# Row sums of squares on TensorE, and first projections begun block by block, in a two-layer hybrid diffusion step

## The chip, the cores and the metric

One NeuronCore of one Trainium2 chip runs the whole program. The metric is the time of one execution on the device in microseconds (us). The engines are named as in the profile: PE is TensorE (PEld its weight loads), DVE is VectorE, ACT is ScalarE, POOL is GpSimd, SP is the engine whose queue issues most of the DMA transfers.

## The reference, cut to what matters

The program is one inference step of a two-layer backbone on 640 tokens (512 latent, 128 context) of width 1024. Each layer starts with

```python
h = rmsnorm(x, prm['norm1_g'][l]) * (1 + sc1) + sh1      # sc1, sh1: slices of silu(cond) @ w_mod + b_mod
cols = jnp.einsum('bnd,de->bne', h, prm['w_in'][l])       # 2832 columns: q, k, v, z, logits, u, vb, pp
# rmsnorm: x * rsqrt(mean(x * x over the 1024 features) + eps) * g
```

and goes on with a gated DeltaNet, a spatial-gating MLP and a pooling branch on slices of `cols`, an output projection, a second norm of the same kind and a SwiGLU FFN. A last norm follows the second layer. Only the first norm of the first layer and the first products behind it are touched here.

## The kernel before, in words

Features lie on the 128 partitions, tokens on the free axis: `xall` holds x as 8 blocks of 128 features x 640 tokens (KT = 8 blocks, NCH = 5 chunks of 128 tokens). float32 products are made as three products of operands split in a rounded part (hi) and a rest (lo): `mm3` issues hi x hi, hi x lo and lo x hi, all through the helper `mm` (L117). The 16 columns of the logits (C_L) need only two products per block, since hi and lo of their weights share one operand. DVE's helpers are `tt` (L122), `stt` (L125) and `ts`; ACT's is `act` (L150).

The norm is applied late. `Norm.add` (L403 to L411) makes block k of x times (gain x (1 + scale)) as `xhi` on ACT and `xlo` on DVE; the products run on that, and each product is multiplied by the row factor `rst` = 1 / sqrt(mean square) as it leaves PSUM. The shift of the modulation rides along as two extra columns in front (`Norm.shift`, L396), so the first half of a product (320 tokens and these two columns) needs the shift, and the second half does not.

The start of the program does this. x is loaded, transposed on PE (L547), positions are added. Then the row statistics: ACT squares the 8 blocks (L580, L582), DVE adds the odd ones into `sb` (L584) and POOL the even ones into `nrm.ss` (L586), and one DVE add joins the two (L587); later `rstd` turns this sum over with five PE transposes (L430), reduces it on DVE (L431) and takes the inverse root. Beside that, the scale half of the modulation is made in two halves of 512 columns (`first_mod_`, L499): 8 float32 products of 32 output rows by 512 columns, placed in four column groups of the array so that four can run side by side; a copy out of PSUM on DVE (`msb`, L505), four PE transposes (L508), a reduce (L510) and two small DVE operations to `sc1` (L591). The first half of the modulation (columns of blocks 0 to 3) is followed in the program by `add` of blocks 0 to 3, the second by `add` of blocks 4 to 7.

Until the shift is there, `early` (L631 to L636) makes the second halves (320 tokens) of four products that do not carry it: logits and first key block, k = 0 to 7, then second key block and first query block, k = 0 to 7. Their weights come from `lgb`, `k0b` and, split at L622 and L623 with a low priority, `k1b` and `q0b`. Then come the row factor (`finish`, L437), the two halves of the shift modulation (L640), the shift columns (L642), and the first halves of the same four products, in `gemm_xs`.

The order of each engine's queue is fixed before the run. A planner takes the instructions by priority (program order, moved by the entries of PRI through `at`) as they become ready in its own account of time; a negative entry means later: `first` +1000, `rst` +80, `add` -100, `kept` -1000. On the chip each engine then runs its queue in that order.

```python
with at("add"):
    nrm.add(k, xks[k], None, shift=False)
```

Of the kernel before, what the change touches and what calls it, by code (L numbers as in the profile page):

```python
# [9 lines left out]
F32 = mybir.dt.float32  # L10
# [6 lines left out]
D = 1024  # L17
P = 128
# [14 lines left out]
# steps of the modulation after each half of a product, by branch  # L33
PUMPS = {'log0': (0, 0), 'k00': (0, 0), 'q00': (1, 2), 'sgu0': (1, 1), 'z0': (0, 1), 'v10': (1, 1), 'q10': (0, 0), 'v00': (1, 0), 'k10': (0, 1), 'pool0': (1, 0)}
# engines of single steps: a ScalarE, v VectorE, p GpSimdE
ENG = {"gul11": "a", "kd10": "a", "conv_k01": "a", "conv_v10": "v", "gul00": "v", "mtc10": "v", "pumpmix0": "a", "kd11": "v", "gul01": "v", "mtc01": "a", "conv_q00": "v", "conv_v00": "v", "kd00": "a", "conv_q10": "a", "conv_k00": "v", "conv_q11": "a", "conv_v01": "a", "conv_v11": "a", "gul10": "a", "kn11": "a", "kn01": "a", "msb": "v", "pumpout0": "a", "dec01": "a", "conv_k11": "a", "dec00": "s", "pumpffn0": "a", "mtc11": "v", "mtc00": "a", "kd01": "a"}
GW, NB = 3, 2
# offsets in the order of issue: > 0 earlier
# [7 lines left out]
def host_constants():  # L46
# [10 lines left out]
    # from here on: not kept on chip as they are  # L57
# [34 lines left out]
def tile_hybrid_step(ctx: ExitStack, tc: tile.TileContext,  # L92
# [40 lines left out]
    def times(key, o, i, c, default):  # L133
        """o = i * c, c one number per row"""
        e = ENG.get(key, default)
        if e == "a":
            act(o, i, AF.Copy, scale=c)
        elif e == "v":
            ts(o, i, c, None, MUL)
        else:  # L140
            nc.gpsimd.tensor_scalar(o, i, c, None, op0=MUL)
# [10 lines left out]
    class at:  # L152
        """the instructions inside come that much earlier in the order of issue"""
# [11 lines left out]
    def behind(ins, prev):  # L165
        """queues one instruction of an engine behind another"""
# [10 lines left out]
    def in_turn(key, ins):  # L177
        """instructions of one kind in the order of the program"""
# [40 lines left out]
    # steps: 512 columns x 128 rows of w_mod; a step's load is issued some steps ahead of its arithmetic  # L219
# [4 lines left out]
    def mod_sums(l, c0, ma):  # L224
# [11 lines left out]
        # sums over the 32 rows of each quarter, then over the quarters  # L236
# [50 lines left out]
    def pump_to(l, w):  # L287
        """until that sixth of the modulation is there"""
# [8 lines left out]
    def wload(parts, kn, n):  # L297
        """parts: [(dram [rows, n], k0, kn)] -> [P, kn, n]"""
# [7 lines left out]
    def wsplit(v):  # L306
        """hi, lo as blocks [P, n]"""
# [32 lines left out]
    def mmk(o, wb, k, xk, sl):  # L340
        """one k block of the products with the scaled residual; 16 columns: hi and lo in one operand"""
# [6 lines left out]
    def gemm_xs(wb, xs, evac, pumps=(1, 1), done=None):  # L348
        """products with the scaled residual; the first half carries two shift columns in front.
        done: the second half's, where it came first."""  # L350
# [28 lines left out]
    def rsqrt(y, a, t):  # L379
        """y = 1 / sqrt(a) for small tiles: bit shift, then three Newton steps; t: scratch like y."""  # L380
# [8 lines left out]
    class Norm:  # L389
        """scaled residual split in two, and the row statistics of the plain one."""  # L390
# [33 lines left out]
        def rstd(self, after=None):  # L424
            """per row: [row in chunk, chunk]"""
            st = sm.tile([P, 3, NCH], F32, tag="st", name="st", bufs=2)
            for q0, q1 in ((4, 5), (0, 4)):
# [5 lines left out]
            ts(st[:, 1], st[:, 1], 1.0 / D, EPS, MUL, ADD)  # L433
# [3 lines left out]
        def finish(self, after=None):  # L437
            r = self.rstd(after)
# [17 lines left out]
    wsp = tc.alloc_tile_pool(name="wsh", bufs=1, side="right")  # L456
    with tc.tile_pool(name="xin", bufs=1) as xp:
# [27 lines left out]
        def first_w(pool, j, c0, kp=KT):  # L485
            """512 columns of w_mod; the row blocks from kp on in the tiles of the later steps"""
# [7 lines left out]
        def first_mod(ws, c0, pool=None):  # L494
            """four row blocks side by side"""
# [40 lines left out]
        # feature rows, positions added  # L536
# [34 lines left out]
        sb = sm.tile([P, NT], F32, tag="rst", name="sb", bufs=1)  # L571
        for k in range(KT):
            xk = xks[k]
            if k % 2:
                sq = xp.tile([P, NT], F32, tag="sq", name="sq", bufs=1)
            else:
                sq = sm.tile([P, 2, 512], F32, tag="ma", name="sq", bufs=1).rearrange("p s n -> p (s n)")[:, 0:NT]
            # sums of squares in two strands
            if k < 2:
                act((nrm.ss, sb)[k], xk, AF.Square)  # L580
                continue
            act(sq, xk, AF.Square)  # L582
            if k % 2:
                tt(sb, sb, sq, ADD)  # L584
            else:
# [851 lines left out]
```

## Time and profile before

| | |
|---|---|
| median of 3 runs | 1740.75 us (1739.99 to 1743.5) |
| span of the profiled execution, first to last instruction | 1737.7 us |
| PE busy | 1666.4 us (96%) |
| DVE, ACT, POOL busy | 1155.2, 761.1, 585.3 us |
| mean granted clock of PE | 0.987 of full |
| DMA | 174.34 MB, mean 100 GB/s |

The page gives the span of the profiled execution and no separate time for it; the median of the runs stands 3.05 us above that span. Times in the rows are microseconds from the span's start: start, duration, engine, line, operation, output <- inputs, shapes and how many instructions were merged; in brackets the idle time before and what ended it. A clock of 1.00 is 2.4 GHz, 0.50 is 1.2 GHz.

### The profile page before, as it was taken

What the parts mean: (1) busy time and instruction counts of PE and PEld (TensorE: products, weight loads), DVE (VectorE), ACT (ScalarE), POOL (GpSimd) and SP (SyncE); (2) the same over time, 40 slices, a digit from 0 to 9 for tenths busy, and PEclk for the clock granted to TensorE, in tenths of its full rate; (3) what the DMA queues carried; (4) which work ended last, traced back from release to release, by engine and by line L of the source; (5) the groups of instructions that cost most, each with busy time, mean ns of one, the idle gap of its engine ahead of it and who ended that gap; (6) DMA issues with size and microseconds to landing.
All of it is one profiled execution on the core that took longest, in us unless ns stands there. A gap on an engine that the chain in (4) does not pass through costs nothing.

```text
span 1737.7 us, 33153 instructions
## 1 busy us (share of the span) xinstructions
PE 1666.4 (96%) x12952; PEld 1603.2 (92%) x12952; DVE 1155.2 (66%) x2462; ACT 761.1 (44%) x1564; POOL 585.3 (34%) x578
## 2 busy tenths in 40 slices
PE   6999999998899999999999999999999999999997
PEld 4788989988899999999998899999999999999997
DVE  6698688799888688877467777675544434433454
ACT  4557765554444344434246656543322212321232
POOL 3342330367645454554164112013411221222110
PEclk8999999999999999999999999999999999999999
DMA  9431231444444544453241211113222222222221
GB/s 316 143 98 57 68 99 29 150 127 139 145 141 141 154 137 143 143 158 103 62 144 52 62 38 50 37 51 126 83 73 74 79 79 74 74 73 73 74 85 61
DMA packets 243379, 174.34 MB, mean 100 GB/s; under 512 B 10006, under 2 KB 212376, under 8 KB 243224
## 3 DMA queue, kind: packets, MB, share of 16 engines
q1 hardware_dynamic: 231888, 157.44, 29.8%
q10 hardware_dynamic: 10184, 12.29, 2.2%
q0 software_dynamic: 1152, 2.51, 0.4%
q8 instruction: 102, 1.67, 0.4%
q14 instruction: 53, 0.43, 0.1%
HBM read 163.29 MB, written 8.91 MB: 99 GB/s over the span
## 4 chain that ended last, share of the span: by engine, by line
PE 53%; DVE 3%; ACT 1%; issue 1%; POOL 0%; DMA 0%; DVEq 0%; POOLq 0%; ACTq 0%
PE acc L117 47%; PE dl L117 5%; DVE wl L122 0%; PE md L117 0%; DMA w<-in_w_down_dram 0%; PE dl L1379 0%; DVE cv L125 0%; POOL guh L830 0%; PE md L760 0%; DVE yt L125 0%; DVE st L125 0%; DVE Z L122 0%; ACT wh L322 0%; ACT MT L945 0%; DVE SI L122 0%
## 5 line engine op out<-in xcount | busy, mean ns | idle before, releaser
L117 PE MATMUL acc<-xhi,wh 128*128 128x322 f32 (+2 forms) x2112 | 667.4, 316 | 5.4 <-DVE ga L122 4.6
L117 PE MATMUL acc<-xlo,wh 128*128 128x322 f32 (+2 forms) x2112 | 666.0, 316 | 1.4 <-DVE xlo L125 1.2
L117 PE MATMUL acc<-xhi,wl 128*128 128x320 f32 (+1 forms) x2080 | 655.0, 315 | 5.1 <-DVE wl L122 5.1
L326 POOL TENSOR_TENSOR wl<-w,wh 128x384 fp32r<-128x384 f32 x188 | 258.7, 1376 | 792.5 <-ACT wh L322 777.9
L117 PEld LDWEIGHTS acc<-xhi,wh 128*128 128x128 f32 (+1 forms) x2112 | 399.4, 189 | 10.7 <-PE acc L117 7.2
L117 PEld LDWEIGHTS acc<-xlo,wh 128*128 128x128 f32 (+1 forms) x2112 | 400.2, 189 | 4.1 <-POOL spp L1148 1.5
L117 PEld LDWEIGHTS acc<-xhi,wl 128*128 128x128 f32 x2080 | 396.4, 191 | 6.6 <-DVE wl L122 5.9
L322 ACT CAST wh<-w 128x1024 fp32r<-128x1024 f32 (+1 forms) x188 | 194.5, 1035 | 343.4 <-PE acc L117 282.6
L282 POOL TENSOR_TENSOR ma<-ma,wm 128x512 f32<-128x512 f32 x140 | 207.2, 1480 | 133.5 <-ACT wm L150 113.8
L122 DVE TENSOR_TENSOR wl<-w,wh 128x640 fp32r<-128x640 f32 (+1 forms) x188 | 213.3, 1134 | 50.5 <-ACT wh L322 23.9
L117 PE MATMUL acc<-ah,wh 128*128 128x320 f32 (+2 forms) x632 | 195.6, 309 | 0.7 <-ACT ah L1322 0.7
L117 PE MATMUL acc<-al,wh 128*128 128x320 f32 (+2 forms) x632 | 195.1, 309 | 0.1
L117 PE MATMUL acc<-ah,wl 128*128 128x320 f32 (+2 forms) x632 | 195.1, 309 | 0.0
L150 ACT ACTIVATE wm<-wm,sc 128x512 f32<-128x512 f32 x140 | 101.1, 723 | 135.0 <-DVE ma L125 117.8
L125 DVE SCALAR_TENSOR_TENSOR x<-acc,mod,x 128x128 f32<-128x128 f32 (+3 forms) x192 | 77.9, 434 | 119.8 <-PE acc L117 119.5
L125 DVE SCALAR_TENSOR_TENSOR ma<-wm,sc,ma 128x512 f32<-128x512 f32 x140 | 134.9, 964 | 25.6 <-DMA wm<-in_w_mod_dram 24.7
L117 PEld LDWEIGHTS acc<-ah,wh 128*128 128x128 f32 x632 | 118.7, 188 | 1.2 <-ACT ah L1322 1.1
L117 PEld LDWEIGHTS acc<-al,wh 128*128 128x128 f32 x632 | 118.7, 188 | 0.3 <-DVE al L122 0.3
L117 PEld LDWEIGHTS acc<-ah,wl 128*128 128x128 f32 x632 | 118.7, 188 | 0.0
L1322 ACT CAST ah<-ga 128x320 fp32r<-128x320 f32 x88 | 40.5, 460 | 155.9 <-DVE ga L125 155.9
L150 ACT ACTIVATE ga<-ga,bt 128x320 f32<-128x320 f32 x132 | 57.4, 468 | 89.9 <-DVE ga L122 89.9
L122 DVE TENSOR_TENSOR ga<-acc,rst 128x320 f32<-128x320 f32 x88 | 42.4, 483 | 73.9 <-PE acc L117 73.4
(369 smaller groups left out, 2481.7 us busy)
## 6 DMA issues: line engine op xcount, KB each, us to landing
w<-in_w_gu_dram SPq DMA_DIRECT2D x88, 512.0 KB, 3.7
wm<-in_w_mod_dram SPq DMA_DIRECT2D x162, 256.0 KB, 2.9
w<-in_w_in_dram SPq DMA_DIRECT2D x44, 512.0 KB, 3.6
w<-in_w_down_dram SPq DMA_DIRECT2D x32, 512.0 KB, 4.2
w<-in_w_out_dram SPq DMA_DIRECT2D x32, 256.0 KB, 3.0
wf<-in_w_mod_dram SPq DMA_DIRECT2D x30, 256.0 KB, 6.5
w<-in_w_down_dram SPq DMA_DIRECT2D x16, 384.0 KB, 3.4
x<-xd ACTq DMA_DIRECT2D x16, 320.0 KB, 4.7
```

Source lines behind the costliest of these rows:

```text
L117: return nc.tensor.matmul(o, lhsT=l, rhs=r, start=st, stop=sp, **kw).ins
L122: recent["v"] = nc.vector.tensor_tensor(o, a, b, op=op).ins
L125: recent["v"] = nc.vector.scalar_tensor_tensor(o, a, s, b, op0=op0, op1=op1).ins
L150: recent["a"] = nc.scalar.activation(o, i, f, **kw).ins
L282: nc.gpsimd.tensor_tensor(ma[:, 1], ma[:, 1], wm, op=ADD)
L322: nc.scalar.copy(wh, v)
L326: nc.gpsimd.tensor_tensor(wl[:, c:], v[:, c:], wh[:, c:], op=SUB)
L1322: nc.scalar.copy(hi[:, sl], ga[:, sl])
```

## The change

The squares are no longer added up elementwise. Each squared block serves as the weights of five float32 products (one for each chunk of 128 tokens) with two columns of ones, all 8 x 5 of them accumulated in one PSUM tile, whose columns then are the row sums in the layout that `rstd` wants; its transposes and reduces fall away for this norm. The second `first_mod` loses its priority of +1000. The products of logits and first key block are issued for k = 0 to 3 between the two halves of the modulation; then second key block and first query block for k = 0 to 3, and both pairs for k = 4 to 7.

```diff
-        def rstd(self, after=None):
+        def rstd(self, after=None, sums=None):
             st = sm.tile([P, 3, NCH], F32, tag="st", name="st", bufs=2)
-            for q0, q1 in ((4, 5), (0, 4)):
+            for q0, q1 in ((4, 5), (0, 4)) if sums is None else ():
...
-            ts(st[:, 1], st[:, 1], 1.0 / D, EPS, MUL, ADD)
+            ts(st[:, 1], st[:, 1] if sums is None else sums, 1.0 / D, EPS, MUL, ADD)
...
-        sb = sm.tile([P, NT], F32, tag="rst", name="sb", bufs=1)
+        pss = dl()[:, 0:2 * NCH]
         for k in range(KT):
-            xk = xks[k]
-            if k % 2:
-                sq = xp.tile([P, NT], F32, tag="sq", name="sq", bufs=1)
-            else:
-                sq = sm.tile([P, 2, 512], F32, tag="ma", name="sq", bufs=1).rearrange("p s n -> p (s n)")[:, 0:NT]
-            if k < 2:
-                act((nrm.ss, sb)[k], xk, AF.Square)
-                continue
-            act(sq, xk, AF.Square)
-            if k % 2:
-                tt(sb, sb, sq, ADD)
-            else:
-                nc.gpsimd.tensor_tensor(nrm.ss, nrm.ss, sq, op=ADD)
-        tt(nrm.ss, nrm.ss, sb, ADD)
+            sq = xp.tile([P, NT], F32, tag="sq", name="sq", bufs=2)
+            act(sq, xks[k], AF.Square)
+            for ch in range(NCH):
+                mm(pss[:, 2 * ch:2 * ch + 2], sq[:, ch * P:(ch + 1) * P], ones[:, 0:2], k == 0 and ch == 0, k == KT - 1 and ch == NCH - 1, skip_group_check=True)
+        ssum = sm.tile([P, NCH], F32, tag="ssum", name="ssum", bufs=1)
+        early = {C_L: (lgb, acc()[0:32, 0:HALF]), C_K: (k0b, acc()[:, 0:HALF])}
+        def early_go(cs, k0, k1):
+            for k in range(k0, k1):
+                for c0 in cs:
+                    mmk(early[c0][1], early[c0][0], k, nrm.xs[k], slice(HALF + 2, XW))
         for j in range(2):
-            first_mod(wsc[j], D + 512 * j, xp)
+            if j == 0:
+                first_mod(wsc[j], D, xp)
+            else:
+                first_mod_(wsc[j], D + 512, xp)
...
                 nc.sync.dma_start(xd[k], xks[k])
+            if j == 0:
+                early_go((C_L, C_K), 0, 4)
+        nc.vector.tensor_copy(ssum, pss.rearrange("p (c t) -> p c t", t=2)[:, :, 0])
...
-                for cs in ((C_L, C_K), (C_K + P, C_Q)):
-                    for k in range(KT):
-                        for c0 in cs:
-                            mmk(early[c0][1], early[c0][0], k, xs[k], slice(HALF + 2, XW))
+                early[C_K + P], early[C_Q] = (k1b, acc()[:, 0:HALF]), (q0b, dl()[:, 0:HALF])
+                early_go((C_K + P, C_Q), 0, 4)
+                early_go((C_L, C_K), 4, KT)
+                early_go((C_K + P, C_Q), 4, KT)
                 with at("rst"):
-                    rst = nrm.finish(split)
+                    rst = nrm.finish(split, ssum)
```

## Rows read from the trace of the kernel before

**Rows 1.** The page: span, and busy time of each engine.

```profile
span 1737.7 us, 33153 instructions
PE 1666.4 (96%) x12952; PEld 1603.2 (92%) x12952; DVE 1155.2 (66%) x2462; ACT 761.1 (44%) x1564; POOL 585.3 (34%) x578
```

**Rows 2.** Windows: PE, PEld, DVE, ACT, POOL busy, then PEclk, DMA share, GB/s.

```profile
20.00:21.00 1.00, 1.00 (x8) 0.00 (x0) 0.55 (x1) 0.42 (x1) 1.00 (x1) 0.53 1.09 345
...
32.00:33.00 1.00, 0.00 (x0) 0.00 (x0) 1.00 (x3) 0.00 (x0) 0.00 (x0) 0.50 0.96 304
...
38.00:39.00 1.00, 1.00 (x9) 0.88 (x8) 1.00 (x3) 1.00 (x4) 0.00 (x0) 1.00 1.03 373
```

**Rows 3.** Timeline of PE from 17 to 56 us.

```profile
17.98 3.36 PE L117 MATMUL md<-wf,sc 128*32 128x512 f32 x16 [1.84 <-ACT sc L150]
22.75 0.66 PE L508 MATMUL md<-r_ident,msb 128*128 128x128 f32 x4 [1.41 <-DVE msb L147]
23.34 4.33 PE L117 MATMUL md<-wf,sc 128*32 128x512 f32 x16
33.41 1.12 PE L508 MATMUL md<-r_ident,msb 128*128 128x128 f32 x4 [5.74 <-DVE msb L147]
...
35.58 0.61 PE L117 MATMUL acc<-xhi,wh 128*32 128x320 f32 x1
...
39.70 0.31 PE L117 MATMUL acc<-xhi,wh 128*32 128x320 f32 x1
...
42.66 0.31 PE L117 MATMUL acc<-xhi,evn 128*128 128x320 f32 x1
...
55.80 0.31 PE L117 MATMUL acc<-xhi,wh 128*32 128x322 f32 x1
```

**Rows 4.** Timeline of DVE, same stretch.

```profile
20.45 1.64 DVE L122 TENSOR_TENSOR sb<-sb,sq 128x640 f32<-128x640 f32 x1 [3.68 <-ACT sq L150]
22.02 0.68 DVE L147 COPY msb<-md 128x512 f32<-128x512 f32 x1
22.90 1.59 DVE L122 TENSOR_TENSOR sb<-sb,sq 128x640 f32<-128x640 f32 x1 [0.20 <-ACT sq L150]
24.41 0.18 DVE L510 TENSOR_REDUCE mod<-md 128x8 f32<-128x32 f32 x1
...
27.77 0.81 DVE L122 TENSOR_TENSOR sb<-sb,sq 128x640 f32<-128x640 f32 x1
...
32.68 0.68 DVE L147 COPY msb<-md 128x512 f32<-128x512 f32 x1
...
35.94 3.79 DVE L125 SCALAR_TENSOR_TENSOR xlo<-xall,sc,xhi 128x512 fp32r<-128x512 f32 x8 [0.52 <-ACT xhi L150]
```

**Rows 5.** Timeline of ACT, same stretch.

```profile
17.82 0.72 ACT L150 ACTIVATE ss<-xall 128x640 f32<-128x640 f32 x1
...
26.25 3.73 ACT L150 ACTIVATE xhi<-xall,sc 128x512 fp32r<-128x512 f32 x8
```

**Rows 6.** Timeline of PE: float32 products alone, narrow ones, and four groups side by side.

```profile
44.07 1.92 PE L117 MATMUL md<-wf,sc 128*32 128x512 f32 x16
...
46.77 1.02 PE L117 MATMUL dl<-ss,cst 128*128 128x512 f32 x2
47.64 0.60 PE L508 MATMUL md<-r_ident,wm 128*128 128x128 f32 x4
...
69.49 0.33 PE L117 MATMUL dl<-g,cst 128*128 128x20 f32 x2
...
70.78 0.40 PE L117 MATMUL acc<-xhi,eon 128*128 128x322 f32 x1
```

**Rows 7.** Window in the first layer's inverse: small products at the lower clock.

```profile
250.50:251.00 0.50, 0.50 (x38) 0.50 (x41) 0.50 (x1) 0.00 (x0) 0.50 (x1) 0.50 0.00 0
```

**Rows 8.** SP's timeline at the last loads for the shift; their time to landing.

```profile
38.10 2.03 SPq L490 DMA_DIRECT2D wm<-in_w_mod_dram  x2
...
DMA to landing us min/median/max: 5.3/5.8/6.2
```

More of the change, by code (lines that the diff above doesn't have):

```diff
@@ L432, in rstd, with finish @@
                                                op=ADD, axis=AX.X).ins, after)
-            ts(st[:, 1], st[:, 1], 1.0 / D, EPS, MUL, ADD)
+            ts(st[:, 1], st[:, 1] if sums is None else sums, 1.0 / D, EPS, MUL, ADD)
             rsqrt(st[:, 0], st[:, 1], st[:, 2])
             return st[:, 0]
-        def finish(self, after=None):
-            r = self.rstd(after)
+        def finish(self, after=None, sums=None):
+            r = self.rstd(after, sums)
             rst = sm.tile([P, NT], F32, tag="rst", name="rst", bufs=1)
@@ L570, in tile_hybrid_step @@
         tt(wsum, wsum, cw3[:, :, 2, :], ADD)
-        sb = sm.tile([P, NT], F32, tag="rst", name="sb", bufs=1)
+        pss = dl()[:, 0:2 * NCH]
         for k in range(KT):
-            xk = xks[k]
-            if k % 2:
-                sq = xp.tile([P, NT], F32, tag="sq", name="sq", bufs=1)
-            else:
-                sq = sm.tile([P, 2, 512], F32, tag="ma", name="sq", bufs=1).rearrange("p s n -> p (s n)")[:, 0:NT]
-            if k < 2:
-                act((nrm.ss, sb)[k], xk, AF.Square)
-                continue
-            act(sq, xk, AF.Square)
-            if k % 2:
-                tt(sb, sb, sq, ADD)
-            else:
-                nc.gpsimd.tensor_tensor(nrm.ss, nrm.ss, sq, op=ADD)
-        tt(nrm.ss, nrm.ss, sb, ADD)
-        for j in range(2):
-            first_mod(wsc[j], D + 512 * j, xp)
+            sq = xp.tile([P, NT], F32, tag="sq", name="sq", bufs=2)
[8 more added lines that the diff above has]
+                    mmk(early[c0][1], early[c0][0], k, nrm.xs[k], slice(HALF + 2, XW))
+        for j in range(2):
+            if j == 0:
+                first_mod(wsc[j], D, xp)
+            else:
+                first_mod_(wsc[j], D + 512, xp)
             with at("first"):
@@ L604, in tile_hybrid_step @@
                 pa_.tile([P, n], F32, tag=tag, name=f"{tag}_", bufs=b)
-            early = {}
             if l == 0:
@@ L630, in tile_hybrid_step @@
                 split = recent["v"]
-                early = {C_L: (lgb, acc()[0:32, 0:HALF]), C_K: (k0b, acc()[:, 0:HALF]),
-                         C_K + P: (k1b, acc()[:, 0:HALF]), C_Q: (q0b, dl()[:, 0:HALF])}
-                for cs in ((C_L, C_K), (C_K + P, C_Q)):
-                    for k in range(KT):
-                        for c0 in cs:
-                            mmk(early[c0][1], early[c0][0], k, xs[k], slice(HALF + 2, XW))
+                early[C_K + P], early[C_Q] = (k1b, acc()[:, 0:HALF]), (q0b, dl()[:, 0:HALF])
+                early_go((C_K + P, C_Q), 0, 4)
+                early_go((C_L, C_K), 4, KT)
+                early_go((C_K + P, C_Q), 4, KT)
                 with at("rst"):
-                    rst = nrm.finish(split)
+                    rst = nrm.finish(split, ssum)
                 for j in range(2):
```

## The prediction

> **What bounds the kernel now.** I began with the page: PE is busy 1666.4 of 1737.7 us [rows 1], so time can come only from places where PE waits or runs slowly, and the 71.3 us in which it is not busy are the whole field. The change touches the start alone, so next I read PE's timeline up to the point at which the first halves of the first products begin, 55.80 us [rows 3]; from there on the program is the same, and whatever this point moves, the end should move with it. I use it as the marker.
>
> In that stretch PE waits once for long: 5.74 us from 27.67 to 33.41, for the copy `msb` of the second half of the scale modulation [rows 3]. DVE's timeline says why: the products behind that copy were done at 27.67, but DVE made it at 32.68, behind the `xlo` of blocks 0 to 3 and two leftover adds of the squares [rows 4]. The windows show the second cost: the clock is 0.50 in this idle time and 1.00 again only from 38 us [rows 2], so the first ten of the early products take twice as long. From 35.58 to 55.80 PE has work without a pause.
>
> **What the change removes.** Four DVE adds go: 1.64, 1.59 and 0.81 us, and a joining one of about 0.81 [rows 4], 4.85 in all. The first two lie on the path: the products of the first half end at 21.34 (17.98 + 3.36), and `msb` starts at 22.02 behind the add; its transposes end at 23.41, and the reduce starts at 24.41 behind the next add [rows 3, 4]. So the first scale could come up to 1.7 us earlier. The last two adds stand among the `xlo` of blocks 0 to 3, ahead of the second `msb`: 1.6 us. POOL's three adds go as well; POOL feeds nothing on this path but a part of the key weights' rest, so I count that at nothing. The five transposes and two reduces of `rstd` go; they were off the path, except for about 1 us of PE ahead of 35.58.
>
> **What it adds.** Forty float32 products with 128 x 128 weights and two columns. The nearest row is six such products with 20 columns: 12 records from 69.49 to 70.78, 0.1075 us each, two records per product [rows 6]. Their price is that of the weight loads, so two columns will hardly be cheaper: 80 x 0.1075 = 8.6 us. This is at the full clock; at half of it, 17.2. I take 8.6, the value of the nearest row, and keep 17.2 for the range; a gain is excluded, since these are instructions that PE did not have. The Trainium skill (TensorE: Matmul & The Clock Gate, section "Back-to-back issue gap") gives an issue floor of about 25 ns to matmuls of 1 to 64 columns; by it the eighty records would take 2.0 us, an estimate. The row above disagrees, and I go by the row.
>
> There is a new wait in both directions. ACT's squares now have two buffers that PE must empty; a square takes 0.72 us [rows 5], its five products 1.08, so PE sets the pace, and behind the waiting square stand the cast of the first key weights and `xhi` of blocks 0 to 3, which begin at 26.25 [rows 5]. Eight sets at 1.08 from 18.5 on end at 27.2 if PE does nothing else. On PE, the new products stand among the 16 + 16 records of the scale modulation and ahead of the first `msb` transposes, wherever the planner put them.
>
> One copy of `ssum` on DVE and the early start of the root are a few operations of 0.2 us whose result is wanted only behind all early products: nothing, covered by at least 5 us of PE work. One of three `dl` tiles is held until that copy; the next user needs one only at about 43: nothing. No DMA is added; SP's order stays. The last shift weights land by 38.10 + 2.03 + 6.2 = 46.3 [rows 8], and a product, copy, transposes and reduce need some 0.87 + 0.68 + 0.60 + 0.18 = 2.3 more [rows 3, 4, 6], so 48.6 is the earliest marker that DMA allows; it does not bind.
>
> **What it moves.** Blocks 0 to 3 of logits and first key block, 20 products, took 35.58 to 39.70, blocks 4 to 7 39.70 to 42.66, 0.148 each [rows 3]. The first group goes into the idle time. Then `add` of blocks 4 to 7 is next in line: its last `xlo` ends at 39.73 (35.94 + 3.79) [rows 4], and less the 1.6 us of the adds and plus five products the last key block cannot be through before 38.9. By the adds alone the second key block, which starts at 42.66, could start 3.7 us earlier.
>
> **The sum.** The question is whether PE has room. From 17.98 until the second key block starts it must do: scale modulation, first half, 3.36; transposes 0.66; second half between 1.92 (as eight products packed four abreast, [rows 6]) and 4.33 (as paced by its loads now, [rows 3]); new products 8.6; transposes 0.60; forty early products at 0.148, 5.9. That is 21.0 to 23.5 us without a pause, so the second key block starts at 39.0 to 41.4 instead of 42.66: 3.6 to 1.2 earlier. I take the end nearer to the present pacing, since the queue is rigid and the second half's products still come one load at a time: **1.2 us earlier**. Spoiled packing works the other way: a product of that shape alone costs 0.87 (46.77 to 47.64) against 0.24 abreast [rows 6], so 16 products, each cut off by new ones, would take 13.9 instead of 7.7, 6.2 more; that gives +5.0. So the bounds are -3.6 and +5.0 at the full clock. Added to the median of 1740.75: **1739.5 us**, with 1737.1 and 1745.8 for the ends. About 0.2%, 3.5 us, is what a measurement of this kernel can tell from no change, so the likeliest case counts as the same.
>
> **The rivals.** *The new products vanish in waits (faster).* If the planner puts them behind the first `msb` transposes, or if they are cheaper than the row says, then the DVE terms count in full: first scale 1.7 earlier, second `msb` at 32.68 - 1.7 - 1.6 = 29.4, everything behind it 3.3 earlier and the 1.2 GHz stretch gone, which cost the first twenty early products 4.1 - 20 x 0.148 = 1.2. That is -4.5: 1736.2. The issue floor of the Trainium skill (same page and section) would lead here too. For it: 5.74 us of idle time lie there, larger than anything else at the start. Against it: the first square is ready at 18.5, just when the first scale products run, and a queue that runs in order has them in front.
>
> *PE falls to the lower clock under them (slower).* The mechanism sits between 18 and 28 us: now the scale products alone raise the clock at 21, having started at 0.50 [rows 2]. Two-column products keep the array's loads busy and stream little, and the row in the first inverse shows PE with 38 small products in half a microsecond, busy all the time, at 0.50 [rows 7]. Each record at 0.50 costs 0.1075 more; from -1.2 it takes 44 of the 80 to come to +3.5, all 80 give +7.4. With 60: +5.2, 1746.0. Against it: the scale products still stand among them.
>
> *The gain is given back (same).* DVE limits PE in places behind the marker, and the first `msb` could come as late as it comes early; then 1740.75. The planner may also order later parts otherwise, with its account of time shifted at the start; no row prices this. I allow 2 us on either side, 3% of the 71.3 in which PE is not busy.
>
> **How the numbers follow.** Forecast, with PE just finding room (-3.4 to +1): 0.45. Vanishing products: 0.20. Lower clock, or packing spoiled in more than half of the cases: 0.17. Given back, about zero: 0.18. Faster by more than 0.2% is the second case with a bit of luck in the later order: 0.21; slower the third: 0.17; the same 0.62. The range leaves out 1 in 10 at either end: 1735.5, the vanishing case with a little more, to 1745.5, just short of the middle of the slow one. The likeliest case alone reaches from 1737.3 to 1741.8.
>
> **What would show it.** In the changed profile: forty products in pairs of records 0.11 us apart between 18 and 30; no DVE or POOL operation on `sq`; PE's idle time before the second `msb` transposes under 2 us instead of 5.74; the first logits product before 33 instead of at 35.58; the second key block between 39 and 42; the marker at about 54.6. I am wrong if the weight loads of the new products last 0.2 us with the clock at 0.50 beyond 24 us, if `xhi` of block 0 starts well behind 26.25 and takes the second `msb` with it, or if the marker moves and the end does not.

## The result and the profile after

The changed kernel takes **1763.89 us**, median of five runs (1762.05 to 1771.67), against 1741.22 us for the kernel before on the same chip: a ratio of 1.0148, 95% interval 1.0128 to 1.0168. The forecast was 1739.5 with a range up to 1745.5. The sign, the size and the range were wrong.

The page of the profile after, span and engines, answers to [rows 1]: the span is 24.4 us longer, and PE's busy time has grown by 25.4 us, so PE does not wait longer, it works longer. DVE's and POOL's shares fell, as the change meant.

```profile
span 1762.1 us, 33299 instructions
PE 1691.8 (96%) x13027; PEld 1620.2 (92%) x13027; DVE 1148.6 (65%) x2457; ACT 761.6 (43%) x1564; POOL 581.9 (33%) x575
```

PE's timeline after, the same stretch as [rows 3]:

```profile
17.62 1.95 PE L117 MATMUL md<-wf,sc 128*32 128x512 f32 x12 [1.72 <-ACT sc L150]
19.50 2.39 PE L117 MATMUL dl<-cst,sq 128*128 128x2 f32 x20
...
26.87 4.43 PE L117 MATMUL dl<-cst,sq 128*128 128x2 f32 x20
31.15 1.09 PE L508 MATMUL md<-r_ident,msb 128*128 128x128 f32 x4
...
45.59 0.66 PE L508 MATMUL md<-r_ident,msb 128*128 128x128 f32 x4 [1.89 <-DVE msb L147]
47.35 0.47 PE L117 MATMUL acc<-xhi,wh 128*32 128x320 f32 x1 [1.11 <-DVE wh L122]
...
50.62 1.05 PE L117 MATMUL md<-wf,sc 128*32 128x512 f32 x4
...
65.81 0.39 PE L117 MATMUL acc<-xhi,evn 128*128 128x320 f32 x1
...
75.30 0.31 PE L117 MATMUL acc<-xhi,wh 128*32 128x322 f32 x1
```

Read it downwards against [rows 3]. The new products (`dl<-cst,sq`) stand ahead of the first `msb` transposes, which come at 31.15 instead of 22.75. They are in five batches, 15.7 us together (2.39 + 2.29 + 4.43 + 4.26 + 2.29). The first early product starts at 47.35 instead of 35.58; the shift products, eight abreast in 1.92 us before [rows 6], now come two or four records at a time, six times about 1.05 us. The second key block starts at 65.81 instead of 42.66, and the marker stands at 75.30, 19.5 us late.

The windows after: from the left the length of the window in us (as in [rows 2] and [rows 7]), PE's busy time in it and its records, the granted clock, the share of the DMA engines, GB/s. PE is busy throughout, and the granted clock is all the same at 0.50, the lower of its two levels (1.2 of 2.4 GHz), from 23 to 43 us.

```profile
19.00:20.00 1.00, 1.00 (x9) 1.00 1.14 339
23.00:24.00 1.00, 1.00 (x6) 0.50 1.05 389
...
42.00:43.00 1.00, 1.00 (x8) 0.50 1.04 383
```

Two more timelines say what stands behind these products. ACT's, after: the squares wait for PE to empty their two buffers, and behind them `xhi` begins at 34.91 instead of 26.25 [rows 5]. Like the clock of 0.50 beyond 24 us, this is a sign by which the prediction called itself wrong.

```profile
29.26 0.74 ACT L150 ACTIVATE sq<-xall 128x640 f32<-128x640 f32 x1 [3.33 <-PE dl L117]
...
34.91 3.71 ACT L150 ACTIVATE xhi<-xall,sc 128x512 fp32r<-128x512 f32 x8
```

DVE's, after: the first `msb` waits 10.46 us for the scale products on PE, the copy of the sums 6.50 us for the last new product; `xlo` follows the copy at 40.90, then the second `msb`, at 44.85 instead of 32.68 [rows 4], and the low part of the logits' weights.

```profile
26.97 0.69 DVE L147 COPY msb<-md 128x512 f32<-128x512 f32 x1 [10.46 <-PE md L117]
...
40.42 0.17 DVE L600 COPY ssum<-dl 128x5 f32<-128x5 f32 x1 [6.50 <-PE dl L117]
...
40.90 0.74 DVE L125 SCALAR_TENSOR_TENSOR xlo<-xall,sc,xhi 128x512 fp32r<-128x512 f32 x1
...
44.85 0.68 DVE L147 COPY msb<-md 128x512 f32<-128x512 f32 x1
...
47.02 0.28 DVE L122 TENSOR_TENSOR wh<-wm,wh 128x128 fp32r<-128x128 f32 x1
```

The marker did not carry the whole loss. I take the start of the same cast of weights on ACT in both profiles and subtract. This **lag** is 19.5 us from the marker to 122 us, 22.0 at 1084 us of the kernel before, and 25.9 from 1152 us on; the last stretch gives 1.5 back. The second step begins with a pause of PE in the second layer, far from the change. PE's timeline after, there:

```profile
1112.52 0.62 PE L117 MATMUL dl<-W 32*32 32x16 f32 x53
1114.66 0.42 PE L117 MATMUL dl<-W 32*32 32x16 f32 x27 [1.51 <-issue]
...
1115.58 1.97 PE L117 MATMUL md<-bnd,qT 128*64 128x128 f32 x16
```

In the kernel before, the same 80 records run through in 0.86 us and the next group takes 1.09:

```profile
1090.48 0.86 PE L117 MATMUL dl<-W 32*32 32x16 f32 x80
...
1091.64 1.09 PE L117 MATMUL md<-bnd,qT 128*64 128x128 f32 x16
```

"Issue" means that the profile shows nothing that PE waited for; behind the pause the clock is at 0.50, and the next group takes 1.97 instead of 1.09.

### The profile page after: what moved, and what is told of

Same layout as the page of the kernel before. It is cut to its first block, busy times and chain, and to the rows that moved or that the text cites. A ratio compares the mean times of both kernels' runs of the same rounds, so it can differ in the third digit from the quotient of the medians.

```text
span 1762.1 us, 33299 instructions
## 1 busy us (share of the span) xinstructions
PE 1691.8 (96%) x13027; PEld 1620.2 (92%) x13027; DVE 1148.6 (65%) x2457; ACT 761.6 (43%) x1564; POOL 581.9 (33%) x575
## 3 DMA queue, kind: packets, MB, share of 16 engines
q0 software_dynamic: 1152, 2.51, 0.4%
## 4 chain that ended last, share of the span: by engine, by line
PE 53%; DVE 3%; issue 1%; ACT 1%; POOL 0%; DMA 0%; DVEq 0%; POOLq 0%; ACTq 0%
PE acc L117 47%; PE dl L117 5%; DVE wl L122 1%; PE md L117 0%; PE dl L1381 0%; POOL guh L832 0%; PE md L762 0%; DVE cv L125 0%; DVE st L125 0%; DVE Z L122 0%; DVE yt L125 0%; DMA w<-in_w_down_dram 0%; DMA x<-xd 0%; DVE SI L122 0%; DVE xlo L125 0%
```

## The experiments

My theory after the first reading: the loss comes from the place of the new products in PE's queue, from the clock under them, and from what follows in the queues of the other engines. Rivals: the order by blocks and the lost priority did it; the copy on DVE did it; the products cost that much wherever they stand. Lags of all profiles against the kernel before, at five points of it (us). A ratio is to the kernel before on the same chip; the runs come from several chips, so ratios compare better than medians. Each lag comes from one profile and strays by up to 1 us, as the row of e2 shows, whose time is that of the kernel before:

| kernel | median | ratio, 95% interval | 95 | 331 | 1084 | 1152 | 1662 |
|---|---|---|---|---|---|---|---|
| changed | 1763.89 | 1.0128 to 1.0168 | 19.5 | 22.1 | 22.0 | 25.9 | 25.9 |
| e1_sums_only | 1769.58 | 1.0131 to 1.0181 | 26.4 | 27.5 | 27.7 | 32.8 | 32.9 |
| e2_blocks_only | 1740.49 | 0.9986 to 1.0004 | -0.5 | -1.0 | 0.3 | -0.4 | -0.4 |
| e3_copy_late | 1767.58 | 1.0137 to 1.0171 | 25.6 | 24.6 | 28.7 | 32.8 | 32.9 |
| e4_cols102 | 1753.38 | 1.0050 to 1.0093 | 10.4 | 10.4 | 11.9 | 14.9 | 15.0 |
| e5_behind2 | 1757.13 | 1.0066 to 1.0100 | 12.4 | 14.7 | 16.0 | 19.8 | 19.8 |
| e5_behind102 | 1748.44 | 1.0030 to 1.0060 | 6.0 | 5.0 | 6.0 | 9.8 | 9.9 |
| e6_moving | 1744.63 | 1.0011 to 1.0031 | 1.4 | 1.9 | 4.7 | 5.3 | 5.4 |
| e8_together | 1752.62 | 1.0043 to 1.0073 | 6.9 | 10.3 | 11.5 | 15.3 | 15.3 |
| e9_before_pad | 1746.92 | 1.0018 to 1.0037 | 1.2 | 2.8 | 7.7 | 10.9 | 10.9 |
| e10_after_pad | 1764.40 | 1.0109 to 1.0138 | 29.7 | 28.4 | 30.6 | 30.4 | 30.4 |
| e11_moving_order | 1736.80 | 0.9962 to 0.9984 | -3.9 | -3.2 | -2.0 | -1.2 | -1.2 |
| e12_moving_order_pad | 1735.68 | 0.9956 to 0.9980 | -2.4 | -4.2 | -2.9 | -3.2 | -3.2 |
| e13_after_pad4 | 1761.79 | 1.0103 to 1.0131 | 19.5 | 17.7 | 18.6 | 18.2 | 18.2 |
| e14_moving_pad4 | 1735.28 | 0.9956 to 0.9980 | -2.6 | -3.3 | -1.9 | -2.4 | -2.4 |

### Which half of the change

**e1_sums_only**, the sums alone:

```diff
-            if j == 0:
-                first_mod(wsc[j], D, xp)
-            else:
-                first_mod_(wsc[j], D + 512, xp)
+            first_mod(wsc[j], D + 512 * j, xp)
...
-            if j == 0:
-                early_go((C_L, C_K), 0, 4)
...
-                early_go((C_K + P, C_Q), 0, 4)
-                early_go((C_L, C_K), 4, KT)
-                early_go((C_K + P, C_Q), 4, KT)
+                early_go((C_L, C_K), 0, KT)
+                early_go((C_K + P, C_Q), 0, KT)
```

> The sums on TensorE alone; the second half of the modulation keeps its priority and the early products are issued in the old order, block by block nowhere. Queue theory (the 40 sums' products stand in PE's queue ahead of the transposes of the first msb and between the shift products, and the copy of their result stands ahead of the residual's low halves on VectorE): the same delay as the whole change, 1761 to 1766 us, marker at 74 to 76 us. Rival, the order by blocks and the lost priority did it: the time of before, 1739 to 1745 us, marker at 54 to 58 us. If each part does half: about 1751 us.

**e2_blocks_only**, the other half alone:

```diff
-        pss = dl()[:, 0:2 * NCH]
+        sb = sm.tile([P, NT], F32, tag="rst", name="sb", bufs=1)
...
+            if k % 2:
+                tt(sb, sb, sq, ADD)
+            else:
+                nc.gpsimd.tensor_tensor(nrm.ss, nrm.ss, sq, op=ADD)
+        tt(nrm.ss, nrm.ss, sb, ADD)
```

> The other half of the change alone: sums of squares added up on VectorE and GpSimd as before, but the second half of the modulation without its priority and the first products block by block. Queue theory: this part changes nothing in the order of PE's queue, 1739 to 1744 us, marker within 1 us of 55.8 us. Rival, the order by blocks did it: 1758 to 1766 us, marker above 70 us.

The sums alone give the whole loss (ratio 1.0156), the blocks alone nothing (0.9995). In e2 the order of PE's queue is that of the kernel before: the first logits product needs `lgb`, whose low part DVE makes behind the second modulation, so there was nothing that blocks 0 to 3 could have started earlier. In e1's profile the first scale products met the clock at 0.50 (12 records in 3.63 us), in the changed kernel's at 1.00 (1.95 us), and e1's lag at the marker is 6.9 us larger. Of these, 1.1 are a later start of the scale products (18.72 against 17.62), and 4.6 more have come by the first transposes (36.84 against 31.15). The changed kernel's own runs spread over 9.6 us; I take the clock at the start for the main reason, but only one of them has a profile, and no run tests it alone.

### The copy of the sums

**e3_copy_late**:

```diff
-        nc.vector.tensor_copy(ssum, pss.rearrange("p (c t) -> p c t", t=2)[:, :, 0])
+        behind(nc.vector.tensor_copy(ssum, pss.rearrange("p (c t) -> p c t", t=2)[:, :, 0]).ins, recent["v"])
```

> The whole change, but the copy of the sums from PSUM to SBUF is queued behind the last low half of the residual on VectorE. Queue theory: the copy held blocks 0 to 3 of the low halves from about 34 to 40.9 us, so these now run before 39 us; what of it reaches the end depends on what is late next (the second msb and the split of the logits' weights): 3 to 6 us less, 1758 to 1761 us. Rival, the copy is harmless because the shift products and the logits' weights end later anyway: 1762 to 1766 us, low halves early all the same.

The copy moved behind all `xlo`, and the first four of these came early, from 40.93 on instead of behind 46.10 in e1, whose scale products also started at the lower clock. Yet the ratio is 1.0154, against 1.0148 for the changed kernel and 1.0156 for e1, and the lag at the marker 25.6 against e1's 26.4; 0.4 of that difference is an earlier start of the scale products (18.32 against 18.72). So the copy's place was worth some 0.4 us there, no more than a lag strays. The rival holds: the copy delays `xlo`, but the logits' weights were later still (53.22 in e3). My expectation of 3 to 6 us missed.

### The clock under the new products

**e4_cols102**, 51 times the columns in the same 40 products:

```diff
-        pss = dl()[:, 0:2 * NCH]
+        pss = dl()[:, 0:102 * NCH]
...
-                mm(pss[:, 2 * ch:2 * ch + 2], sq[:, ch * P:(ch + 1) * P], ones[:, 0:2], k == 0 and ch == 0, k == KT - 1 and ch == NCH - 1, skip_group_check=True)
+                mm(pss[:, 102 * ch:102 * ch + 102], sq[:, ch * P:(ch + 1) * P], ones[:, 0:102], k == 0 and ch == 0, k == KT - 1 and ch == NCH - 1, skip_group_check=True)
...
```

> The whole change with 102 columns of ones instead of 2 in each of the sums' products (the same weights, the same number of products; 51 times the columns). If the fall of the granted clock to 0.50 from 23 to 43 us came from products with few columns: the clock stays at 1.00 there, a product costs 0.23 to 0.35 us, the stretch of sums ends 4 to 8 us earlier and the kernel is at 1752 to 1760 us. Rival, the clock falls whatever the columns are, or the float32 columns cost what the clock gives: 1762 to 1775 us and 0.50 in the same stretch.

More columns made the kernel faster: the ratio fell from 1.0148 to 1.0072 (medians 1763.89 and 1753.38), although in e4's profile the scale products started at the lower clock (12 records in 3.63 us). PE's timeline of e4, one batch: 30 records in 3.60 us, the same 0.12 us each that the two-column products cost at the full clock (2.39 for 20).

```profile
30.52 3.60 PE L117 MATMUL dl<-cst,sq 128*128 128x102 f32 x30
```

The planner put some of e4's products elsewhere, so place and clock are mixed in it. The next pair separates them. Both hold the squares in eight buffers, put all 40 products behind the last scale product and ahead of the second `msb` transposes, and keep PE's order of the kernel before behind that; they differ in the columns alone. On DVE the copy of the sums goes behind the last `xlo`. The diff, cut, for two columns:

```diff
+            if c0 == D + 512:
+                sum_products(m)
...
+                if c0 == D + 512:
+                    behind(tr, recent["sum"])
...
+        def sum_products(m):
+            for k in range(KT):
+                for ch in range(NCH):
+                    m_ = mm(pss[:, 2 * ch:2 * ch + 2], sqs[k][:, ch, :], ones[:, 0:2], k == 0 and ch == 0, k == KT - 1 and ch == NCH - 1, skip_group_check=True)
+                    behind(m_, m)
+                    m = m_
+            recent["sum"] = m
...
+        behind(nc.vector.tensor_copy(ssum, pss.rearrange("p (c t) -> p c t", t=2)[:, :, 0]).ins, recent["v"])
```

> The 40 products as the change has them (squares as weights, 2 columns), but squares in eight buffers, and in PE's queue all 40 behind the last scale product and ahead of the transposes of the second msb, where PE was idle for 5.74 us; everything behind them in the order of before. Place theory (most of the loss came from where they stood, among the scale products, and from the order that followed): 9.3 us at full clock to 17.8 us at half clock against 5.7 us of idle time, so 3.6 to 12 us over before, 1745 to 1753 us. Rival, the loss is the products' own price and their clock, wherever they stand: 1758 us or more.

> The same place and order, with 102 columns in each of the 40 products. Clock theory (products with 2 columns let the granted clock fall, the same products with 102 columns do not): granted clock 1.00 through them, 40 x 0.235 us = 9.4 us, second transposes at about 37 us, 1743 to 1747 us, and below the run with 2 columns by up to 8 us. Rival: the same time as with 2 columns.

PE's timeline of e5_behind2:

```profile
28.59 14.90 PE L117 MATMUL dl<-cst,xna 128*128 128x2 f32 x80
43.36 1.09 PE L515 MATMUL md<-r_ident,msb 128*128 128x128 f32 x4
```

The windows of PE in e5_behind2:

```profile
30.00:31.00 1.00, 1.00 (x11) 1.00 1.17 301
33.00:34.00 1.00, 1.00 (x7) 0.50 1.00 375
```

PE's timeline of e5_behind102:

```profile
28.21 9.18 PE L117 MATMUL dl<-cst,xna 128*128 128x102 f32 x80
37.22 0.60 PE L515 MATMUL md<-r_ident,msb 128*128 128x128 f32 x4
```

The windows of PE in e5_behind102:

```profile
30.00:31.00 1.00, 1.00 (x12) 1.00 1.14 327
33.00:34.00 1.00, 1.00 (x12) 1.00 1.00 361
```

Both enter the products at the full clock, and in both PE is busy all the time. With two columns the clock falls to 0.50 on the way, with 102 it stays: 14.90 against 9.18 us for the products, 6.4 us at the marker (lags 12.4 and 6.0), medians 1757.13 and 1748.44. My ranges for both (1745 to 1753, 1743 to 1747) were too low and the rival's bound for e5_behind2 (1758) just not reached, so either view holds in part: with the products in this place 12.4 of the changed kernel's 19.5 us at the marker remain, and the place takes 7.1 away. Another 7.4 us of e5_behind2's lag come behind its marker.

Even at the full clock 6.0 us remain, and these are not all the price of the products. They do take 9.18 us where 5.74 were idle, so the second transposes come at 37.22 instead of 33.41. But the early products catch up: the second key block starts at 43.72, only 1.1 us later than before. Then PE waits. PE's timeline of e5_behind102 again:

```profile
43.72 0.31 PE L117 MATMUL acc<-xhi,evn 128*128 128x320 f32 x1
...
47.18 0.41 PE L117 MATMUL acc<-xhi,edT 128*128 128x320 f32 x1 [3.00 <-DVE edT L122]
```

DVE's timeline of e5_behind102 shows these weights behind the copy of the sums and the early root:

```profile
42.96 0.16 DVE L615 COPY ssum<-dl 128x5 f32<-128x5 f32 x1
...
46.30 1.29 DVE L122 TENSOR_TENSOR edT<-w,evn 128x640 fp32r<-128x640 f32 x2
```

And DVE's timeline of the kernel before, where they stand ahead of the root:

```profile
39.65 1.28 DVE L122 TENSOR_TENSOR edT<-w,evn 128x640 fp32r<-128x640 f32 x2
```

Behind the wait the clock is at 0.50 (49 to 51 us). So most of the 6.0 us stands behind a place in DVE's queue. That is read from the rows; no run moves the root alone.

### The order behind

**e8_together** is e4 with the shift products, their copies and the kept weights held in the order of the kernel before:

```diff
+                if c0 < D:
+                    behind(m, recent[("go", C_Q, 1 + c0 // 512)])
...
+            if c0 < D:
+                behind(nc.vector.tensor_copy(msb, pm).ins, split)
...
+                if c0 < D:
+                    behind(tr, recent[("go", C_Q, 2 + c0 // 256)])
```

> The kernel with 102 columns from before (sums' products among the scale products, clock at 1.00), with the shift products, their transposes and the split of the kept weights held in the order that the kernel before had (eight shift products abreast, kept weights ahead of the first shift copy). Knock-on theory (the shift products issued one or two at a time cost about 1.0 us each pair, some 6 us in all, and the late kept weights the rest): 4 to 7 us below the 1753.4 us of that kernel, 1746 to 1750 us. Rival, the order behind the second modulation is idle time filled: within 1.5 us of 1753.4 us.

The eight shift products run abreast again (1.92 us), and the lag after the marker is 6.9 instead of 10.4. But at 331 us it is 10.3 against 10.4, and the medians differ by 0.8 us. My expectation (1746 to 1750) missed and the rival, a time within 1.5 us of e4's, held. The 3.5 us were real at the marker and given back between 130 and 331 us: 1.5 behind a pause of PE of 1.30 us at 149 us, 1.1 in the first layer's inverse near 265 us, where the mean clock is 0.74 against 0.91 in e4, and some 0.7 from 300 us on. How much of that the new order caused stays open.

### The sums the other way round

**e6_moving** makes the squares the moving operand, with 32 columns of ones as weights, four products abreast, and sums up the four groups with five small products:

```diff
+                g = 32 * (k % 4)
+                for o, c in ((pss[g:g + 32, 0:512], slice(0, 4)), (ps2[g:g + 32, 0:128], slice(4, 5))):
+                    m_ = mm(o, ones[:, 0:32], sqs[k][:, c, :], k < 4, k >= KT - 4, tile_position=(0, g))
...
+            nc.scalar.copy(nrm.ss[:, 0:512], pss)
+            nc.scalar.copy(nrm.ss[:, 512:NT], ps2[:, 0:128])
...
+                    behind(mm(p5[:, 2 * ch:2 * ch + 2], nrm.ss[:, ch * P:(ch + 1) * P], ones[:, 0:2], ch == 0, ch == NCH - 1, skip_group_check=True), recent[("go", C_K, 7)])
...
```

> The sums the other way round: 32 columns of ones as weights and the squares as the moving operand, four products abreast in four row groups (16 products, as the scale products are issued), then a copy on ScalarE and five small products behind the early products; queue order of before. If the price of the weights (128 rows of squares for 2 columns) was what made the sums dear: 16 products in about 2.5 us, inside the 5.74 us of idle time, and the adds that left VectorE now give their gain: second transposes 1 to 2.5 us before 33.41 us, 1736 to 1740 us. Rival, sums on PE cost whatever their form: 1743 us or more; or the freed time is taken back before the marker: 1740 to 1742 us.

PE's timeline of e6:

```profile
28.40 2.68 PE L117 MATMUL dl<-xna,cst 128*32 128x512 f32 x30
31.21 0.66 PE L515 MATMUL md<-r_ident,msb 128*128 128x128 f32 x4
...
52.49 1.12 PE L515 MATMUL md<-r_ident,wm 128*128 128x128 f32 x4 [3.38 <-DVE wm L510]
```

The sums now take some 3 us (28.00 to 31.08), and their five small products 1.17 us more, at 37.77 behind the early products. The transposes come 2.2 us earlier, and the second key block at 38.80 instead of 42.66. By its median e6 could pass for the first rival (1743 or more), but the rows show a gain that goes again: PE stands for 3.38 us before the second shift transposes, and its marker is at 57.10. DVE's timeline of e6 names the queue:

```profile
51.06 0.48 DVE L122 TENSOR_TENSOR lgT<-acc,rst 32x320 f32<-32x320 f32 x1 [7.55 <-DMA S<-in_state_delta_dram]
...
51.75 0.68 DVE L510 COPY wm<-md 128x512 f32<-128x512 f32 x1
```

And ACT's timeline of e6 (ACTq are the DMA issues in its queue):

```profile
45.97 1.16 ACTq L1028 DMA_DIRECT2D S<-in_state_delta_dram  x2
47.51 2.72 ACTq L1167 DMA_DIRECT2D bnd<-in_consts_dram  x2
50.27 0.75 ACT L445 COPY rst<-dl 128x512 f32<-128x512 f32 x2 [11.93 <-DMA xd<-xall]
```

The evacuation `lgT` waits for `rst`, a copy on ACT that stands behind DMA issues in ACT's queue, and these wait in turn for the stores of `xall`. In e6 the planner put `lgT` ahead of the second shift copy; in the kernel before the copy went first.

**e11_moving_order** puts that order back:

```diff
+                if l == 0 and half == 1:
+                    behind(recent["v"], recent["shift"])
```

> The kernel with the squares as moving operand, with the first logits evacuation on VectorE queued behind the second shift copy and its sums, as it was in the kernel before. In that kernel the evacuation, which waits for ScalarE's copy of the row factors until 50.3 us, held the second shift copy to 51.75 us and PE's transposes to 52.49 us. Theory: the shift copy at about 47.2 us, transposes at 48 us, no idle 3.38 us on PE, marker at 52.5 to 54 us against 57.1 us; 3 to 4.5 us off that kernel: 1740 to 1742 us, the jump near 1095 us still in. Rival, the marker is held by something else (the evacuation itself frees the bank that the marker's products need): marker 55 us or later, 1743 us or more.

PE's timeline of e11:

```profile
48.43 0.60 PE L515 MATMUL md<-r_ident,wm 128*128 128x128 f32 x4
...
51.80 0.31 PE L117 MATMUL acc<-xhi,wh 128*32 128x322 f32 x1
```

The marker is at 51.80, 4.0 us before the old 55.80, and the kernel takes 1736.80 us, ratio 0.9973: one queue position on DVE was worth 5.3 us at the marker (57.10 in e6) and 7.8 us in the medians, which come from two chips (ratios 1.0021 and 0.9973). It beats both kernels, by more than I expected (1740 to 1742).

### The pause in the second layer

Counting PE's records by start, the longest pause of the changed kernel, the 1.51 us at 1114.66, stands ahead of record 8432. In e1, e3, e4, both e5 and e8 a pause of 1.45 to 1.74 us stands ahead of 8432 or 8433 as well; the other pauses over 0.1 us in these seven profiles stand ahead of 976, 1104, 2372, 7418 and 7546, within one record, with one exception (0.15 us ahead of 12789, in e5_behind2). The kernel before has pauses too, of 0.20 us at 260.0 (ahead of 2246), 0.48 at 1097.8 (8560) and 0.66 at 1694.3 (12714); the changed kernel has no pause at the last place, and it is there that the last stretch gives back some of the lag. The places are the same whatever runs there, and neighbours (976 and 1104, 7418 and 7546) are 127 or 128 records apart. The change adds 75 records, so other instructions meet these places. What holds PE at them no run shows. Two runs test whether the place decides, one on each kernel. **e9_before_pad** puts 37 unused small products (74 records) into PE's idle time of the kernel before:

```diff
+            if c0 == D + 512:
+                pp = dl()
+                for i in range(37):
+                    m = mm(pp[0:32, 0:16], ident[0:32, 0:32], ident[0:32, 0:16], True, True)
...
```

> The kernel before, with 37 small products (32x32 weights, 16 columns, result unused; 74 records) put into PE's idle time ahead of the second msb's transposes, so that all later PE instructions stand about as many places further on as in the changed kernel (75 records). Position theory (PE pauses at fixed places of its instruction stream, and in the changed kernel one of these places falls into the 80 small products near 1114 us): marker within 1 us of 55.8 us, no change up to about 1080 us, a pause of 1.3 to 1.8 us at record 8432 and 3 to 5 us more from there to the end: 1743.5 to 1746.5 us. Rival, the jump at 1100 us comes from something else in the change (the later start, the transfers): 1740 to 1742 us and no pause there.

**e10_after_pad** puts 26 of them (52 records, 127 with the change's) ahead of the changed kernel's first scale product:

```diff
+        pp = dl()
+        for i in range(26):
+            recent["pad"] = mm(pp[0:32, 0:16], ident[0:32, 0:32], ident[0:32, 0:16], True, True)
```

> The changed kernel with 26 such small products (52 records) ahead of its first scale product, where PE waits for ScalarE anyway: the stream then stands 127 records further on than before, one distance between two pauses, so that the pauses fall where they fell before. Position theory: no jump near 1110 us, 3 to 5 us less than the changed kernel from there on, 1757 to 1761 us if the clock starts at 1.00 there (the profile tells the offset on either side of 1110 us whatever the start). Rival: the jump stays.

PE's timeline of e9, in the second layer:

```profile
1098.07 0.64 PE L117 MATMUL dl<-W 32*32 32x16 f32 x54
1100.44 0.49 PE L117 MATMUL dl<-W 32*32 32x16 f32 x26 [1.72 <-issue]
...
1101.48 1.98 PE L117 MATMUL md<-bnd,qT 128*64 128x128 f32 x16
```

The kernel before, with nothing of the change in it, shows the pause at the predicted record and loses 5.7 us in the median (1746.92, just above my range), 3.2 of the lag there. I missed that its lag grows before that too: 2.1 us behind two pauses at 140 and 144 us (0.85 and 1.17 us), and 4.6 us from 400 to 420 us (2.8 to 7.4), which are no such pause: PE waits 4.38 us at 408.53 for a part `wl` of the weights that DVE makes (1.23 us before), DVE in turn waits 1.78 us for a load of `w_mod`, and the clock is at 0.50 behind it. Whether the added records brought that about is open, and the profiled run (1749.10) is the slowest of its ten. In e10 one pause over 0.1 us is left (0.18 us at 1723.5) and the lag is flat across 1110 us (30.6, 30.4), as expected; but its added products ran one after another and took 2.95 us on the path, so the median (1764.40, expected 1757 to 1761) did not tell it.

**e13_after_pad4** spreads them over four tiles, abreast; **e12_moving_order_pad** and **e14_moving_pad4** do the same (45 products, 90 records) for e11, one after another and abreast. For e13, against e10:

```diff
-            recent["pad"] = mm(pp[0:32, 0:16], ident[0:32, 0:32], ident[0:32, 0:16], True, True)
+            q, u = 32 * (i % 4), 16 * (i // 4)
+            recent["pad"] = mm(pp[q:q + 32, u:u + 16], ident[q:q + 32, q:q + 32], ident[q:q + 32, q:q + 16], True, True, tile_position=(q, q))
```

> The changed kernel with the 26 small products spread over four tiles, abreast, ahead of the first scale product. Position theory: no pause near 1110 us, and with the added products inside PE's wait of 1.8 us the time falls below the changed kernel's 1763.9 us by the jump, 3 to 5 us: 1758 to 1762 us. Rival, the pauses only move time that is lost elsewhere: 1763 to 1766 us.

> The same with 45 small products (90 records) ahead of the first scale product, so that PE's stream stands 127 records further on than in the kernel before. Both theories together: marker at 52.5 to 54 us and no jump near 1095 us: 1736 to 1739 us, faster than both kernels. If only the position theory holds: about 1740 us; if neither: 1743 us or more.

> The kernel with the squares as moving operand, the shift copies ahead of the first evacuation and 45 small products abreast on four tiles. Position theory: no pauses, and the front no longer held by the added products (4.98 us before, some 1 to 2 us now, of which 1.84 us is idle): 1731 to 1735 us. Rival, the front is late all the same because the start of the scale products is set by ScalarE: 1735 to 1737 us.

PE's timeline of e13: the added products, then the clock at 1.00 for the first scale products, as in the changed kernel's profile, and the marker at the same place.

```profile
16.09 0.63 PE L117 MATMUL dl<-r_ident 32*32 32x16 f32 x52
17.87 1.91 PE L117 MATMUL md<-wf,sc 128*32 128x512 f32 x12 [1.16 <-ACT sc L150]
...
75.23 0.31 PE L117 MATMUL acc<-xhi,wh 128*32 128x322 f32 x1
```

From the same lag at the marker (19.5) the changed kernel goes to 25.9, e13 to 18.2: **7.7 us** apart. The changed kernel's 6.4 us come mostly in three steps: 1.3 behind two pauses at 158 and 162 us (0.30 and 0.94 us), 0.9 in the first layer's inverse, 3.9 at the pause near 1110 us. e13 has none of these pauses. In the inverse neither has one, but the mean clock is 0.74 in the changed kernel (265 to 285 us) and 1.00 in e13, and 2.3 of the 7.7 us come there. The medians say less: 1761.79, the ratio falls from 1.0148 to 1.0117 with intervals that overlap, and e13's profiled run (1756.56) is the fastest of its four. So the pauses are shown to move with the count of records; what they cost in the median is some 5 us, an estimate from the two ratios. For e11 the median gains 1.1 us (e12), with the ratios' intervals overlapping; the rows tell more, since e11's lag climbs from -3.9 to -1.2 and e12's stays near -3. e14 has e12's ratio, 0.9968: its rival held, ACT and the loads set the start of the scale products anyway. At 0.9968 (0.9956 to 0.9980) these two have the lowest ratios of all the kernels, though not clear of e11's.

## Why the prediction was wrong

**The removed adds: right, and hidden.** No DVE or POOL operation on `sq` is left. Their 3.3 us could not show, since the first `msb` now waits 10.46 us for PE; in e11, where the sums fit, the second transposes come 2.7 us earlier (30.70) and the marker 4.0.

**The price of the new products: this step failed.** "I take 8.6, the value of the nearest row": they took 15.7. The row itself was good: 0.115 us a record at the full clock (9.18 / 80) against 0.1075. The Trainium skill (TensorE: Matmul & The Clock Gate, section "LDWEIGHTS (loading the stationary operand)") has a rule that fits this price: a weight load lasts as long as the weights have columns, at 1.2 per ns, so 107 ns for 128, an estimate by the page. The trace is near it at the full clock, 0.115, and not at 0.50, where a record took 0.213 (4.26 / 20). The issue floor of about 25 ns of the Trainium skill (same page, section "Back-to-back issue gap") was rightly set aside. What failed is the clock at which I took the row. That the two-column products would let it fall was my second rival, with 0.17 and 1746.0; [rows 7] showed the case, and e5 shows the mechanism: 14.90 against 9.18 us for the products, 6.4 us at the marker. "The scale products still stand among them" was no argument: with them among the products the clock fell too.

**Room on PE: this step failed more.** "The queue is rigid" was right, and against the sum. I added up the work from 17.98 to the second key block as if it could run without a pause, 39.0 to 41.4; it came at 65.81. In that queue the new products stand ahead of the first transposes, the squares behind PE's pace, `xhi`, `xlo`, the second `msb` and the logits' weights behind them. I had named the waits one by one and not the chain that they form. Spoiled packing I priced for the scale products; it hit the shift products: 6.3 us in six pieces instead of 1.92.

**"The first group goes into the idle time": failed.** It needed weights that DVE makes behind the second modulation, 35.14 before and 47.02 after. e2 shows that this half of the change moved nothing.

**The copy and the early root, counted at nothing: this failed, but cost the changed kernel little.** The copy stood ahead of all `xlo`; e3 shows that this was worth some 0.4 us at most, because the logits' weights were later. I called both covered because their result is wanted late, and did not ask what stands behind them on DVE: in e5_behind102 that is `edT`, and PE waits 3.00 us for it.

**"From there on the program is the same": failed.** The stream of instructions was the same, its places were not. 2 us was my allowance for later parts; 6.4 us were added behind the marker, most of them at pauses that e13 does not have.

Of the 25.9 us, then, by differences between lags of single profiles: 6.0 for the products at the full clock (e5_behind102: 1.1 up to the second key block, the rest behind the wait for its weights), 6.4 for the clock under them (e5_behind2 less that), 7.1 for their place and the order that follows (19.5 less 12.4; 14.0 by e1, which like e5_behind2 starts at the lower clock), and 6.4 behind the marker. The parts were not added one at a time to one kernel, so the split is rough. I had looked for "slower" in one mechanism at a time, and several came together.

## What to carry to other kernels

A sum over rows is cheap on TensorE when the data moves and the ones are the weights (16 products, some 3 us); with the data as weights it cost 14.9 us for two columns, at the lower clock, and 9.2 for 102. Work that is moved to an engine with idle time must be pinned to that idle time in its queue, and the queues of the others checked for what then stands behind it: e6 and e11 differ in one position on VectorE and in 5.3 us at the marker. Before a change of a few tenths of a per cent is judged, look for pauses without a releaser far away from it: more instructions alone can move them (e9, 0.28% slower, though not all of that stands at pauses).

## What the hardware showed that I had not expected

PE at a busy share of 1.00 for 20 us at a granted clock of 0.50, and the same products with 102 instead of 2 columns at 1.00: more columns, at the same price per record, made the kernel faster. And pauses of 0.1 to 1.7 us at fixed places of PE's stream of records: one of 1.51 us among many small products cost 3.9 us of lag, with the lower clock behind it (1.97 us instead of 1.09 for the next group). With 127 records more than the kernel before nearly all of them are gone; what holds PE there no run shows.
